# Level scores of a chunked gated recurrence: one 128x128 product a chunk, or two of 64 keys by 64 queries on separate column tiles

## The chip, the cores and the metric

The kernel runs on one core of a Trainium2 chip. The metric is the device time of one execution in microseconds (us). TensorE multiplies matrices into PSUM (the profile calls its products PE and its weight loads PEld), VectorE (DVE) and ScalarE (ACT) read PSUM and do elementwise work, GpSimd (POOL) works on SBUF alone, and SyncE (SP) issues most DMAs.

## The reference, cut to what matters

The program is one layer of a transformer-like block on 2048 latent tokens of width 1024 with a context of 256 tokens. One of its two head groups is a gated linear recurrence, run in both directions, with 4 heads of 128 channels:

```python
def chunk_gla(q, k, v, log_f, h0):
    # S_t = diag(f_t) S_{t-1} + k_t v_t^T,  o_t = S_t^T q_t
    ...
        b = jnp.cumsum(gc, axis=2)
        o_inter = jnp.einsum('bhtk,bhkv->bhtv', qc * jnp.exp(b), h)
        diff = b[:, :, :, None, :] - b[:, :, None, :, :]
        decay = jnp.where(mask, jnp.exp(jnp.where(mask, diff, 0.0)), 0.0)
        scores = jnp.einsum('bhtk,bhsk,bhtsk->bhts', qc, kc, decay)
        o = o_inter + jnp.einsum('bhts,bhsv->bhtv', scores, vc)
...
    o_f, h_f = chunk_gla(q, k_f, v, logf_f, h0_f)
    o_b, h_b = chunk_gla(flip_t(q), flip_t(k_b), flip_t(v), flip_t(logf_b), h0_b)
    o = rmsnorm(o_f + flip_t(o_b), hg_gain.reshape(HG_HEADS, 1, HG_DIM))
```

Around it stand an input projection (1024 to 3584 columns), a gated unit with a 128x128 mixing matrix, an output projection, and a gated MLP with a 3x3 convolution. All is computed in float32 accuracy.

## The kernel before, in words

**Stages.** The kernel first makes the modulation vectors and the context states, then runs the input projection for two halves of 1024 tokens, and beside it the recurrence (up to about 925 us), then the output projection, the MLP's up projection with the convolution, and the down projection. The large products are split in a high and a low part of type float32r (three products for one); those of the recurrence use plain float32, which TensorE runs as two passes, each with a weight load.

**The recurrence.** The function `hg` handles one head of one half: 1024 tokens as 8 chunks of 128 (`NCH`). It is called 8 times (2 halves, 4 heads). The scores inside a chunk are built by levels B = 1, 2, 4, ..., 64 (`LV`). At level B, two neighbouring blocks of B tokens look at each other: forward for one direction, backward for the other. The pair of blocks is 2B wide, so with B up to 32 a pair lies in the first or in the second 64 tokens of the chunk, and with B = 64 the two halves of the chunk look at each other. The tile `Q` holds the queries of both directions in two rows of 1024, and a level reads for each token the row that it needs. The tile `K` holds in its row 0 the keys that the level needs. A level's steps are

- 8 products `T.matmul(o, K[:, 0, chunk], view(Q, ...))`, one a chunk: 128 keys by 128 queries, contracted over 128 channels, four to a PSUM bank with the tag `sc` (two banks);
- for B below 64, `copy_predicated` on VectorE, one for each group of four chunks: it takes from the bank what the level's mask `msk` selects and puts it in the tile `sc` in SBUF. For B = 64 two ScalarE copies a group take the two off-diagonal quarters;
- `level_update` on VectorE, which multiplies `Q` by the decay totals `tot` of the level, `level_keys` on VectorE, GpSimd and ScalarE, which makes the keys of the next level in another `K` tile, and `next_tot`.

Level B = 1 is computed otherwise, as column sums of elementwise products with ones.

**Order.** The tile framework sets semaphores from what each instruction reads and writes, and may reorder instructions that are not kept in place by `pin`. The order of TensorE is mostly written out by hand: `run_banks` issues the projections (28 or so between two levels), and after each three products it calls `slot()`, which lets two queues of generators (`Pump`) go one step when they are due. `hg` is such a generator. What counts as due is reckoned by the planner's clock `T.t`, which the class `Tensor` moves on by an estimated price of each product; `yield 4.2` means that the next level is issued when 4.2 us of estimated products have been issued since. The background queue (`bg_q`: modulation blocks, the preparation of the output and down projections' weights, with their DMAs) uses the same clock.

Of the kernel before, what the change touches and what calls it, by code (L numbers as in the profile page):

```python
# [10 lines left out]
F32R = mybir.dt.float32r  # L11
# [5 lines left out]
DRAM = bass.MemoryType.DRAM  # L17

P = 128
D = 1024  # L20
NK = D // P
SEQ = 2048
TH = SEQ // 2
NCH = TH // P
CTX = 256
HW = 512
NH = 4
FF = 2816
NF = FF // P
GW = 64  # L30
# [9 lines left out]
def level_masks():  # L40
    i = np.arange(P)
    m = []
    for b in LV:
        same = (i[:, None] // (2 * b)) == (i[None, :] // (2 * b))
        opp = (i[:, None] // b) != (i[None, :] // b)
        m.append(same & opp)
    m.append(np.eye(P, dtype=bool))
    return np.ascontiguousarray(np.stack(m, 1).reshape(P, 8 * P).astype(np.float32))


def view(t, off, dims):

    return bass.AP(t.tensor, t.offset + off, [list(t.ap[0])] + [list(d) for d in dims])


class Tensor:
# [5 lines left out]
    def matmul(self, out, lhsT, rhs, **kw):  # L62
        n = 1
        for _, count in rhs.ap[1:]:
            n *= count
        self.t += n / 2400 + 0.0135 if rhs.dtype == F32R else 2 * max(0.112, n / 1200 + 0.005)
        return self.engine.matmul(out, lhsT, rhs, **kw)  # L67

    def transpose(self, out, in_, identity):
# [16 lines left out]
def tile_trunk(ctx, tc, x, c, cx, c_ctx, w_ada, b_ada, norm_mix, norm_ffn, w_in, hg_norm, sgu_g, sgu_b,  # L86
               w_sp, b_sp, w_out, w_up, conv_w, conv_b, w_down, norm_final, masks, out):
    nc = tc.nc
    V, S, G, T = nc.vector, nc.scalar, nc.gpsimd, Tensor(nc.tensor)
# [25 lines left out]

    g_d = dr.tile([2, D], F32, name="g_d")
    oT_d = [dr.tile([P, NK, TH], F32, name=f"oT{hh}") for hh in range(2)]
    xh_d = dr.tile([P, NK, TH], F32, name="xh_d")
    xl_d = dr.tile([P, NK, TH], F32, name="xl_d")
    wo_d = dr.tile([P, NK, 2, D], F32, name="wo_d")  # L120
    wd_d = [dr.tile([P, 2, D], F32, name=f"wd{j}") for j in range(NF // 2)]
    xn_d = [dr.tile([P, D], F32, name=f"xn{i}") for i in range(2 * NCH)]

# [68 lines left out]
    with es1:  # L192
# [8 lines left out]
        msk = pm.tile([P, 8, P], U8, name="msk")  # L201
# [4 lines left out]
        def bank(tag):  # L206
            return ps.tile([P, 512], F32, tag=tag, name=tag, bufs={"pj": 3, "sc": 2, "mi": 3}[tag])
# [7 lines left out]
        def raw_tile():  # L215
            return p1.tile([P, D], F32, tag="raw", name="raw", bufs=3)

# [123 lines left out]
        with tc.manual_schedule():  # L341
# [29 lines left out]
            for k in range(NK):  # L371
                for i in range(2):
                    o = (k % 2) * 256 + i * P
# [130 lines left out]
        def level_update(arr, W, B, tot, kk):  # L504

            n = W // (2 * B)
            nb = W // B
            o = view(arr, 0, [[2 * B, n], [W + B, 2], [1, B]])
            if kk:
                t = view(tot, nb + 1, [[2, n], [-(nb + 1), 2], [0, B]])  # L510
            else:
                t = view(tot, 1, [[2, n], [nb - 1, 2], [0, B]])
            if B < 4 and not kk:
                o = view(arr, 0, [[W + B, 2], [2 * B, n], [1, B]])
                t = view(tot, 1, [[nb - 1, 2], [2, n], [0, B]])
            V.tensor_mul(o, o, t)

        def next_tot(tot, W, B):
            nb = W // B
            od = B in (1, 4, 16, 64)  # L520
            t2 = ph.tile([P, 2 * (W // (2 if od else 4))], F32, tag=f"T{int(od)}", name="tot")
            t2 = t2[:, :nb].rearrange("p (d n) -> p d n", d=2)
            pin(V.tensor_mul(t2, tot[:, :, 0::2], tot[:, :, 1::2]))  # L523
            return t2
# [52 lines left out]
        def level_keys(K, B, tot, K2=None):  # L577

            W, nb = TH, TH // B
            K2 = K2 if K2 is not None else pk.tile([P, 2, W], F32, tag="K", name="K2", bufs=2, align_bytes=AL)  # L580
            if B == P // 2:
                n = W // (2 * B)
                src = [[2 * B, n], [B, 2], [1, B]]
                t = view(tot, nb + 1, [[2, n], [-(nb + 1), 2], [0, B]])
                V.tensor_mul(view(K2, 0, [[2 * B, n], [W + B, 2], [1, B]]), view(K, 0, src), t)
                S.copy(view(K2, W, [[2 * B, n], [B - W, 2], [1, B]]), view(K, W, src))
                return K2
            n = W // (4 * B)
            for row, (o, step, t0, ts) in enumerate(((0, 3 * B, nb + 1, 1 - nb), (B, B, 0, nb + 3))):
                src = [[4 * B, n], [step, 2], [1, B]]  # L590
                e = G if row and B > 1 else V
                keep = pin if B == 1 else lambda i: i
                e.tensor_mul(view(K2, row * W + o, src), view(K, o, src), view(tot, t0, [[4, n], [ts, 2], [0, B]]))  # L593
                o2, step2 = (B, B) if row == 0 else (0, 3 * B)
                src = [[4 * B, n], [step2, 2], [1, B]]
                keep(S.copy(view(K2, row * W + o2, src), view(K, W + o2, src)))
            return K2
# [59 lines left out]
        for h in range(NH):  # L657
            F, K, vt = sets[h % 2]
# [129 lines left out]
        def column_sums(to, hi, lo):  # L788

            T.matmul(to, ones_r, hi, start=True, stop=False)  # L790
            T.matmul(to, ones_r, lo, start=False, stop=True)

        def hg(hh, h, F, K, qs, vt, sgt):
            Q = ph.tile([P, 2, TH], F32, tag="Q", name="Q", align_bytes=AL)
# [10 lines left out]
            pbs = [bank("sc") for g in range(2)]  # L805
# [3 lines left out]
            sc = ph.tile([P, NCH, P], F32, tag="S", name="sc")  # L809
# [15 lines left out]
            yield 3.2  # L825
            tot = F
            for l, B in enumerate(LV):
                dims = [[2 * B, P // (2 * B)], [TH + B, 2], [1, B]]
                if B < 4:
                    dims = [[TH + B, 2], [2 * B, P // (2 * B)], [1, B]]  # L830
                if B == P // 2:
                    dims = dims[1:]
                for g in range(0, NCH, 4):
                    pb = bank("sc")
                    if B == 1:
                        column_sums(pb, knh[g // 4], knl[:, g * P:g * P + 512])
                    for i in range(4) if B > 1 else ():
                        off = (g + i) * P
                        o = pb[:, i * P:(i + 1) * P]
                        if B < 4:  # L840
                            o = view(pb, i * P, [[B, 2], [2 * B, P // (2 * B)], [1, B]])
                        T.matmul(o, K[:, 0, off:off + P], view(Q, off, dims), start=True, stop=True)
                    if B == P // 2:
                        pq = pb.rearrange("p (c t) -> p c t", t=P)
                        S.copy(sc[:B, g:g + 4, B:], pq[:B, :, B:])
                        S.copy(sc[B:, g:g + 4, :B], pq[B:, :, :B])
                        continue
                    V.copy_predicated(sc[:, g:g + 4, :], view(msk, l * P, [[0, 4], [1, P]]),
                                      pb.rearrange("p (c t) -> p c t", t=P))
                level_update(Q, TH, B, tot, False)  # L850
                K, K2 = level_keys(K, B, tot, K2), None
                tot = next_tot(tot, TH, B)
                yield 4.2
# [3 lines left out]
            for d in range(2):  # L857
                for g in range(0, TH, 512):
                    pt = bank("mi")
                    for i in range(4):  # L860
                        o = g + i * P
# [29 lines left out]
            for g in range(0, NCH, 4):  # L891
                po = bank("mi")
                for i in range(4):
                    ch = g + i
                    sl = slice(ch * P, (ch + 1) * P)
                    o = po[:, i * P:(i + 1) * P]
# [127 lines left out]
        def head(hh, h):  # L1024
# [31 lines left out]
            def post():  # L1056
                hg_q.add(marked(hg(hh, h, t["F"], t["K"], t["qs"], t["vt"], t["sgt"]), (hh, h, "end")))
                if hh == 1:
                    hg_q.add(deferred(h))
# [102 lines left out]
        i = len(seq) - 4  # L1162
# [11 lines left out]
        for n in range(2):  # L1174
            sl = slice(n * 512, n * 512 + 512)
            for k in LATE:
                t = wo[k][:, :, sl]
# [11 lines left out]
    pb = ctx.enter_context(tc.tile_pool(name="pb", bufs=1, reuse_waits="tile"))  # L1189
# [11 lines left out]
    def zbank():  # L1201
        turn[1] += 1
        return ps2.tile([P, 512], F32, tag=f"uz{turn[1] % 2}", name="uz")
# [75 lines left out]
    for n, (u, i) in enumerate(prods):  # L1279
        m = units.index(u) + 2  # L1280
# [12 lines left out]
    with tc.tile_pool(name="po", bufs=1, reuse_waits="tile") as po:  # L1293
# [59 lines left out]
        for t, (hh, g) in enumerate(tiles):  # L1353
# [12 lines left out]
            o = ops.pop(t)  # L1366
# [33 lines left out]
    B = [[xah[:, i] if i < NR else None, xal[:, i] if i < NR - 1 else None] for i in range(7)]  # L1400
# [186 lines left out]
    for n, (u, i) in enumerate(prods):  # L1587
# [10 lines left out]
        p = zbank() if i == 1 else u.z if i in (4, 6) else u.x  # L1598
        hi, lo = u.A[i]
        order = [(k, 0, t) for k in range(4) for t in range(2)] + [(k, 1, 0) for k in range(4)]  # L1600
        for m, (k, w, t) in enumerate(order):
            T.matmul(p, (hi, lo)[w][:, k, :], B[i][t][:, k, :], start=(m == 0 and i in (0, 1, 4)),
                     stop=(m == len(order) - 1), skip_group_check=True)
# [36 lines left out]
    V = Kept(nc.vector, pin)  # L1640
# [191 lines left out]
    for n in range(3, 7 * NJ - NB):  # L1832
        q, j = divmod(n, NJ)
# [54 lines left out]
```

## Time and profile before

| | |
|---|---|
| median of three runs | 2432.91 us (2429.09 to 2433.07) |
| profiled execution, its time and its span | 2434.68 us, span 2432.9 us |
| TensorE products, weight loads (busy) | 2398.8 us, 1991.8 us |
| VectorE, ScalarE, GpSimd (busy) | 1658.5 us, 1045.1 us, 868.8 us |
| level products `sc<-Q,K` | 768 passes, 94.2 us busy |
| masked copies `sc<-msk,sc` | 96, 67.7 us busy |

Rows of groups read: line of the kernel, engine, operation, tile written <- tiles read, shape, xcount | busy time in us, mean ns of one | idle time of the engine before them and what ended it. For TensorE `128*64` would be rows by columns of the array. In order of time the columns are start, busy time, engine, line, operation; rows of the same kind that follow each other are merged with xcount. Durations of products overlap each other, so the pace is read from starts. The line of a product is that of the helper in `Tensor`, so products are told apart by their tiles.

### The profile page before, as it was taken

The page shows a single profiled execution, that of the slowest core. Times are in us where ns is not written, and L with a number is a line of the kernel's source. Part 1 is how long each engine was busy: PE and PEld are TensorE (multiplying, and loading weights), DVE is VectorE, ACT ScalarE, POOL GpSimd, SP SyncE. Part 2 cuts the span into 40 slices and gives each one's busy share as a digit, 9 for nine tenths or more (in the row PEclk, how much of TensorE's full clock was granted, in tenths as well). Part 3 has the DMA queues.
Part 4 walks back from the last instruction along what each step waited for, and adds up shares of the span by engine and source line. Part 5 has one row for each costly group of instructions (what it writes and reads, how often), then busy time and mean ns, then how long its engine had stood idle before and what let it go on. Part 6 is the DMA issues. An engine that isn't in the chain of part 4 may idle for free.

```text
span 2432.9 us, 32291 instructions
## 1 busy us (share of the span) xinstructions
PE 2398.8 (99%) x11711; PEld 1991.8 (82%) x11711; DVE 1658.5 (68%) x2251; ACT 1045.1 (43%) x1803; POOL 868.8 (36%) x788
## 2 busy tenths in 40 slices
PE   8999999999999999999999999999999999999998
PEld 5887887888888887887788888888888888888887
DVE  5757795755786786566596666639866673676876
ACT  4554344443444443454554444434445443332243
POOL 1021110110121122000688778787888870000002
PEclk9999999999999999999999999999999999999999
DMA  8365444463355234678922222563222239834745
GB/s 308 119 205 166 148 143 165 140 225 107 119 193 171 91 105 145 217 218 254 301 85 89 93 81 91 185 230 97 86 94 84 86 108 387 285 118 147 229 152 199
DMA packets 304046, 393.28 MB, mean 162 GB/s; under 512 B 32634, under 2 KB 215682, under 8 KB 300814
## 3 DMA queue, kind: packets, MB, share of 16 engines
q1 hardware_dynamic: 300596, 390.46, 48.0%
q8 instruction: 92, 1.51, 0.2%
q10 hardware_dynamic: 3289, 0.76, 0.1%
q14 instruction: 69, 0.56, 0.1%
HBM read 283.60 MB, written 107.55 MB: 161 GB/s over the span
## 4 chain that ended last, share of the span: by engine, by line
PE 47%; issue 2%; POOL 1%; ACT 0%; DVE 0%; DMA 0%; POOLq 0%; SPq 0%; ACTq 0%
PE ux L67 19%; PE dn L67 15%; PE uz L67 14%; POOL rr L1748 0%; DMA raw<-in_w_up_dram 0%; POOL Al L135 0%; POOL ra L1747 0%; POOL ra L1745 0%; ACT jk L1736 0%; POOL raw L1262 0%; DVE odd L82 0%; POOL raw L1260 0%; DVE dn L1453 0%; POOL s L1258 0%; POOL fl L1258 0%
## 5 line engine op out<-in xcount | busy, mean ns | idle before, releaser
L1453 DVE SCALAR_TENSOR_TENSOR dn<-gp,taps,dn 128x1024 f32<-128x1024 f32 x352 | 448.3, 1285 | 97.7 <-ACT dn L1450 93.3
L67 PE MATMUL dn<-thl,mhl 128*128 128x512 f32 x1680 | 381.0, 389 | 0.0
L67 PEld LDWEIGHTS dn<-thl,mhl 128*128 128x128 f32 x1680 | 315.2, 188 | 65.6 <-issue 0.2
L135 POOL TENSOR_TENSOR Al<-raw,Ah 128x512 fp32r<-128x512 f32 x264 | 341.2, 1309 | 69.4 <-ACT Ah L134 41.0
L67 PE MATMUL pj<-xh,whi 128*128 128x512 f32 x896 | 362.6, 405 | 0.0
L67 PE MATMUL pj<-xl,whi 128*128 128x512 f32 x896 | 352.6, 393 | 0.0
L67 PE MATMUL pj<-xh,wlo 128*128 128x512 f32 x896 | 351.2, 392 | 0.4 <-DVE wlo L135 0.4
L134 ACT CAST Ah<-raw 128x512 fp32r<-128x512 f32 x264 | 163.0, 620 | 240.5 <-PE ux L67 125.0
L67 PE MATMUL ux<-xah,Ah 128*128 128x512 f32 x528 | 205.7, 390 | 0.3 <-ACT keep L1517 0.3
L67 PEld LDWEIGHTS pj<-xh,wlo 128*128 128x128 f32 x896 | 168.6, 188 | 35.9 <-DVE wlo L135 0.8
L67 PEld LDWEIGHTS pj<-xh,whi 128*128 128x128 f32 x896 | 168.9, 189 | 33.7 <-issue 3.5
L67 PEld LDWEIGHTS pj<-xl,whi 128*128 128x128 f32 x896 | 169.2, 189 | 30.8 <-DVE xl L254 0.8
L67 PE MATMUL dn<-wo,o 128*128 128x512 f32 x768 | 182.4, 394 | 0.0
L67 PE MATMUL uz<-yf,Ah 128*128 128x512 f32 x704 | 174.0, 389 | 0.0
L593 POOL TENSOR_TENSOR K<-K,tot 128x512 f32<-128x512 f32 x40 | 61.5, 1538 | 302.7 <-DVE tot L523 156.2
L67 PEld LDWEIGHTS dn<-wo,o 128*128 128x128 f32 x768 | 142.1, 188 | 29.0
L67 PE MATMUL ux<-yf,Ah 128*128 128x512 f32 x528 | 155.4, 389 | 0.0
L67 PEld LDWEIGHTS uz<-yf,Ah 128*128 128x128 f32 x704 | 132.1, 188 | 27.4
L67 PE MATMUL ux<-xah,Al 128*128 128x512 f32 x528 | 141.8, 390 | 1.3 <-POOL Al L135 1.3
L67 PE MATMUL ux<-xal,Ah 128*128 128x512 f32 x352 | 137.0, 389 | 0.0
L1745 POOL TENSOR_SCALAR ra<-ss 128x1 f32<-128x1 f32 x8 | 3.2, 397 | 359.5 <-ACT jk L1736 359.5
L135 DVE TENSOR_TENSOR wlo<-raw,whi 128x1024 fp32r<-128x1024 f32 x67 | 82.5, 1232 | 67.7 <-ACT whi L134 66.3
(344 smaller groups left out, 4449.9 us busy)
## 6 DMA issues: line engine op xcount, KB each, us to landing
raw<-in_w_up_dram SPq DMA_DIRECT2D x88, 512.0 KB, 3.6
mr<-m SPq DMA_DIRECT2D x85, 512.0 KB, 5.4
raw<-in_w_in_dram SPq DMA_DIRECT2D x68, 512.0 KB, 4.8
sT<-wd SPq DMA_DIRECT2D x88, 256.0 KB, 5.0
raw<-in_w_ada_dram SPq DMA_DIRECT2D x32, 512.0 KB, 4.5
yf<-yd SPq DMA_DIRECT2D x14, 1024.0 KB, 10.0
m<-cv SPq DMA_DIRECT2D x22, 544.0 KB, 2.7
raw<-in_w_down_dram SPq DMA_DIRECT2D x22, 512.0 KB, 3.6
```

Of the source, the lines that this page charges most:

```text
L67: return self.engine.matmul(out, lhsT, rhs, **kw)
L134: keep(S.copy(hi, raw))
L135: (eng or G).tensor_sub(lo, raw, hi.bitcast(F32))
L593: e.tensor_mul(view(K2, row * W + o, src), view(K, o, src), view(tot, t0, [[4, n], [ts, 2], [0, B]]))
L1453: V.scalar_tensor_tensor(out=cr, in0=gt[:, t // 3:t // 3 + RH, t % 3:t % 3 + GW], scalar=taps[:, t * NF + f:t * NF + f + 1], in1=cr, op0=A ...
L1745: G.tensor_scalar(out=a, in0=ss, scalar1=plus, scalar2=None, op0=ALU.add)
```

## The change

For each chunk and level above B = 1 the one product becomes two, r = 0 and 1: 64 keys (from e = 64 r) by 64 queries, written to the 64 partitions of PSUM from e on. Its output columns are those of the same half of the chunk for B below 64, and of the other half for B = 64; the two other quarters of the 128x128 block are not computed any more. An output that starts at partition 64 uses the upper half of TensorE's columns, one at partition 0 the lower half. Both banks of a level are asked for first, then come the products of both groups of chunks, then the copies. The masked copy of a group becomes two, each of the quarter on the diagonal (64 partitions by 4 x 64 elements); for B = 1 and B = 64 the copies stay. The planner's price of a float32 product now has its constant part scaled with the number of weight columns.

```diff
+HB = 64
...
-        self.t += n / 2400 + 0.0135 if rhs.dtype == F32R else 2 * max(0.112, n / 1200 + 0.005)
+        m = lhsT.ap[-1][1] / P
+        self.t += n / 2400 + 0.0135 if rhs.dtype == F32R else 2 * max(0.112 * m, n / 1200 + 0.005)
...
             for l, B in enumerate(LV):
-                dims = [[2 * B, P // (2 * B)], [TH + B, 2], [1, B]]
-                if B < 4:
-                    dims = [[TH + B, 2], [2 * B, P // (2 * B)], [1, B]]
-                if B == P // 2:
-                    dims = dims[1:]
+                pbs = [bank("sc") for g in range(2)]
                 for g in range(0, NCH, 4):
-                    pb = bank("sc")
+                    pb = pbs[g // 4]
                     if B == 1:
                         column_sums(pb, knh[g // 4], knl[:, g * P:g * P + 512])
                     for i in range(4) if B > 1 else ():
-                        off = (g + i) * P
-                        o = pb[:, i * P:(i + 1) * P]
-                        if B < 4:
-                            o = view(pb, i * P, [[B, 2], [2 * B, P // (2 * B)], [1, B]])
-                        T.matmul(o, K[:, 0, off:off + P], view(Q, off, dims), start=True, stop=True)
+                        for r in range(2):
+                            off, e = (g + i) * P, r * HB
+                            c = e if B < HB else HB - e
+                            dims = [[2 * B, HB // (2 * B)], [TH + B, 2], [1, B]]
+                            d = e
+                            if B < 4:
+                                dims = [[TH + B, 2], [2 * B, HB // (2 * B)], [1, B]]
+                            if B == HB:
+                                dims, d = [[1, B]], (TH + B) * (1 - r)
+                            o = pb[e:e + HB, i * P + c:i * P + c + HB]
+                            if B < 4:
+                                o = view(o, 0, [[B, 2], [2 * B, HB // (2 * B)], [1, B]])
+                            T.matmul(o, K[:, 0, off + e:off + e + HB], view(Q, off + d, dims), start=True, stop=True)
+                for g in range(0, NCH, 4):
+                    pq = pbs[g // 4].rearrange("p (c t) -> p c t", t=P)
                     if B == P // 2:
-                        pq = pb.rearrange("p (c t) -> p c t", t=P)
                         S.copy(sc[:B, g:g + 4, B:], pq[:B, :, B:])
                         S.copy(sc[B:, g:g + 4, :B], pq[B:, :, :B])
                         continue
-                    V.copy_predicated(sc[:, g:g + 4, :], view(msk, l * P, [[0, 4], [1, P]]),
-                                      pb.rearrange("p (c t) -> p c t", t=P))
+                    if B == 1:
+                        V.copy_predicated(sc[:, g:g + 4, :], view(msk, l * P, [[0, 4], [1, P]]), pq)
+                        continue
+                    for e in (0, HB):
+                        q = slice(e, e + HB)
+                        V.copy_predicated(sc[q, g:g + 4, q], view(msk[q], l * P + e, [[0, 4], [1, HB]]), pq[q, :, q])
```

## The prediction

> **What bounds the kernel now.** I read the page first, then the stretch in which the level scores run, then the groups by shape, and last the order of time around single bursts. From the page:
>
> ```profile
> span 2432.9 us, 32291 instructions
> PE 2398.8 (99%) x11711; PEld 1991.8 (82%) x11711; DVE 1658.5 (68%) x2251; ACT 1045.1 (43%) x1803; POOL 868.8 (36%) x788
> PE   8999999999999999999999999999999999999998
> PEclk9999999999999999999999999999999999999999
> ```
>
> TensorE is busy in every slice at its full granted clock. So what TensorE saves anywhere ends the program earlier, unless another engine makes it wait. The heads of the recurrence lie between 215 and 925 us; the busy time of each engine in that stretch, and what TensorE waited for before level scores there:
>
> ```profile
> 215.00:925.00 710.00, 701.33 (x3888) 599.13 (x3886) 518.48 (x774) 297.04 (x561) 111.04 (x99) 1.00 0.43 144
> PE sc L67 <- DVE K L593: 2.5, 4, 0.9
> PE sc L67 <- DVE Q L516: 1.4, 2, 0.9
> ```
>
> The columns are length, then PE, PEld, DVE, ACT, POOL, clock, DMA share and GB/s. TensorE idles 8.7 us of 710 here, and only six waits, 3.9 us, stand before level scores. VectorE is at 73%, so it has room. The groups that the change touches:
>
> ```profile
> L67 PE MATMUL sc<-Q,K 128*128 128x128 f32 x768 | 94.2, 275 | 3.9 <-DVE K L593 2.5 <-DVE Q L516 1.4
> L67 PEld LDWEIGHTS sc<-Q,K 128*128 128x128 f32 x768 | 92.4, 191 | 9.5 <-issue 4.2 <-ACT whi L134 1.1 <-PE mi L71 1.1
> L848 DVE COPY_PREDICATED sc<-msk,sc 128x512 f32<-128x512 uint8 x96 | 67.7, 735 | 13.4 <-PE sc L67 13.3
> ```
>
> Six levels (B=2 to 64) of eight heads with eight chunks are 384 products; the trace has 768 rows, so an f32 product is two passes, each with its own weight load. 768 rows in 48 levels are 16 passes a level. Durations overlap, so a price has to come from starts. One such burst in order of time, TensorE first, then its weight loads (start, busy, what):
>
> ```profile
> 268.67 0.39 PE L67 MATMUL pj<-xl,whi 128*128 128x512 f32 x1
> 268.89 0.39 PE L67 MATMUL pj<-xh,wlo 128*128 128x512 f32 x1
> 269.12 1.95 PE L67 MATMUL sc<-Q,K 128*128 128x128 f32 x16
> 270.82 0.48 PE L67 MATMUL pj<-xh,whi 128*128 128x512 f32 x1
> 271.14 0.40 PE L67 MATMUL pj<-xl,whi 128*128 128x512 f32 x1
> 271.37 0.39 PE L67 MATMUL pj<-xh,wlo 128*128 128x512 f32 x1
> ...
> 268.90 1.98 PEld L67 LDWEIGHTS sc<-Q,K 128*128 128x128 f32 x16
> ```
>
> The 16 passes already stand in one row. From their first start to the next projection is 1.70 us, and that projection is followed after 0.32 us where 0.23 is usual. A burst therefore takes 1.79 us out of the projections, 0.112 us a pass, and 48 bursts cost 86 us, 3.5% of the run. That is the most the change could touch.
>
> **The change part by part.**
>
> *Streaming.* Each pass of 128 queries becomes two of 64 queries. At half the columns I price one at 0.056 us, half of 0.112. A level has 32 of them in place of 16, so one after the other they cost 32 x 0.056 = 1.79 us, the same as now. A gain comes only if the lower tile (partitions 0 to 63) and the upper one (64 to 127) work at the same time.
>
> *Weight loads.* Would they limit it? In this row the products have two columns to stream:
>
> ```profile
> 35.94 1.05 PE L67 MATMUL sc<-ones_r,acc 128*128 128x2 f32 x8
> L67 PE MATMUL sc<-ones_r,acc 128*128 128x2 f32 x16 | 2.1, 254 | 0.0
> ```
>
> Eight of them take 1.05 us and the last 0.25, so they start (1.05 - 0.25)/7 = 0.114 us apart, though there is next to nothing to stream: loading 128 columns of f32 weights alone holds the pace. Loads and streams are thus equal limits today, and the change loads the same 128 columns a pass in two halves. It halves the burst only if loads of the two tiles overlap as well as streams. No row shows two products on different column tiles. The bounds are full overlap (16 steps of 0.056 us, 0.90 us a burst) and none (32 steps, 1.79).
>
> I take overlap. The program's order helps: within a tile the second pass waits for the first, but the next instruction is for the other tile, so from the second pass on one pass of each tile can run beside one of the other: 17 steps instead of 16, 17 x 0.056 = 0.95 us. And the nearest rows on loads, those of the one-column products below, show two loads in hand (of one tile) before the first of their products is done.
>
> By the Trainium skill, TensorEngine Tiling (Array Packing), Key Properties, different tiles can execute weight loads and products in parallel; by that sentence the sum is the one I take. The trace has no such pair, so it neither bears this out nor refutes it.
>
> *Going into the narrow mode and out.* The nearest rows are the products with one weight column, between projections of 128 (TensorE, then loads):
>
> ```profile
> 368.97 0.39 PE L67 MATMUL pj<-xl,whi 128*128 128x512 f32 x1
> 369.19 0.39 PE L67 MATMUL pj<-xh,wlo 128*128 128x512 f32 x1
> 369.51 1.02 PE L67 MATMUL mi<-acc,ones_r 128*1 128x512 f32 x2
> 370.46 0.50 PE L67 MATMUL pj<-xh,whi 128*128 128x512 f32 x1
> 370.80 0.39 PE L67 MATMUL pj<-xl,whi 128*128 128x512 f32 x1
> 371.03 0.39 PE L67 MATMUL pj<-xh,wlo 128*128 128x512 f32 x1
> ...
> 369.51 0.09 PEld L67 LDWEIGHTS mi<-acc,ones_r 128*1 128x1 f32 x2 [0.35 <-issue]
> 370.46 0.19 PEld L67 LDWEIGHTS pj<-xh,whi 128*128 128x128 f32 x1 [0.86 <-issue]
> 370.57 0.19 PEld L67 LDWEIGHTS pj<-xl,whi 128*128 128x128 f32 x1
> L67 PE MATMUL mi<-acc,ones_r 128*1 128x512 f32 x8 | 4.1, 590 | 0.0
> ```
>
> In: 0.32 us from 369.19 to 369.51 where 0.23 is usual, 0.09 lost. Out: the second pass starts at 369.51 + 1.02 - 0.59 = 369.94, 0.43 after the first; the projection follows 0.52 later, again 0.09 lost. That projection's load starts only with it (370.46), not under the product before, so the next comes after 0.34 instead of 0.23: 0.11 lost. I add 0.06 for the first 64-column load of a burst, half of that 0.11. Together 0.35 us for each of 48 bursts, 16.8 us in all. The ends are 0 (if two tiles of 64 need no change of mode) and 0.35. Both groups of chunks stand in one row before and after, so that edit changes nothing here.
>
> By the same page of the Trainium skill and the same section, changing the tiling mode drains TensorE. The three lost pieces above agree with that; without the rule the sum would lose its 16.8 us.
>
> *Sum on TensorE.* A burst goes from 1.79 to 0.95 + 0.35 = 1.30 us: 0.49 us less, 48 times, 23.5 us.
>
> *Copies.* For B=2 to 32 two masked copies of 128x512 become four of 64x256: 80 instructions become 160; those of B=1 and the ScalarE copies of B=64 stay. What VectorE did after a burst, and a group with 256 columns that also reads PSUM:
>
> ```profile
> 265.35 1.34 DVE L848 COPY_PREDICATED sc<-msk,sc 128x512 f32<-128x512 uint8 x2
> 266.59 1.21 DVE L516 TENSOR_TENSOR Q<-Q,tot 128x1024 f32<-128x1024 f32 x1
> L251 DVE TENSOR_SCALAR xfl<-mi,a,s 128x256 f32<-128x256 f32 x32 | 16.9, 538 | 8.4 <-PE mi L71 4.3 <-ACT sp L253 3.1 <-POOL sp L254 0.8
> ```
>
> Two copies take 1.34 us; the second adds 1.34 - 0.74 = 0.60. The bounds for four halves are 1.34 (half the price) and 4 x 0.53 = 2.1 (the 256-column row, 16.9/32). I take 1.5, near the first, since these copies follow each other without idle time: +0.16 us for 40 levels, 6 to 7 us of VectorE. VectorE's 73% covers it. Behind the copies in VectorE's queue stands the update of Q, and for that the next burst waits. Also, a shorter burst hides less of the first copies: its second half was 0.9 us and becomes about 0.5, so the update comes some 0.6 us later, counted from the burst's end. Here it ended at 267.8 and the next burst began at 269.12, so 1.3 us of slack cover it; of 48 bursts six had none. 6 x 0.6 is 3.6 us; the ends are 0 and that, I take 2.
>
> *Planner.* Its price of a product goes from 0.224 to 2 x 0.1167 = 0.233, which is 0.075 us a level and 3.6 us over the heads. Later steps, with their DMAs on SP's queue and GpSimd's work, are issued slightly earlier relative to the projections. I cost it at nothing; it could move the 8.7 us of waits either way.
>
> **Sum.** The profiled execution took 2434.7 us with a span of 2432.9; its time is 1.8 above the median of the runs, 2432.9. 2434.7 - 23.5 + 2 = 2413.2; against the median 2411. With its own bounds (no price for the mode: 16 us less; a third of the overlap lost or more waiting: 9 us more) this case reaches from 2395 to 2420.
>
> **Rivals.**
>
> *Tiles take turns (the other sign).* If the weight loads of the two tiles queue on one path, 32 steps of 0.056 us remain, 1.79 us, and the change of mode comes on top: +0.35 us a burst, 16.8 us, and 2 for the waits: 2452 against the median, and 2456 if a half pass costs 0.058, as the planner has it. For it: the row with two columns, where loads alone hold 0.114 us. Against it: two loads in hand at 369.51. The point that decides is the mean step: 1.79 = 0.35 + 32 x 0.045, so overlap must bring a half pass below 0.045 us to gain anything.
>
> *Loads exposed.* If a load could not run under a product of the same rows, each half pass would pay load and stream, 0.11 us: 32 x 0.112 + 0.35 - 1.79 = 2.1 us a burst, 102 us, 2537. Against it: at 268.90 a load starts 0.01 us after a product that uses all 128 rows.
> The Trainium skill, TensorE: Matmul & The Clock Gate, Part 3, states that loads overlap products in flight only when the row group differs; that would give this rival. The row at 268.90 speaks against it, at least for untiled products.
>
> *VectorE takes the gain back.* If every burst, not six, waited 0.6 us for the update of Q, 29 us would go and the time would be 2438, no gain. It decides when the slack falls under 0.6 us in most bursts; 42 of 48 without any wait and the 1.3 us above speak against it.
>
> **How the numbers follow.** Overlap 0.52; taking turns 0.33; partial overlap or VectorE's return, around no change, 0.10; exposed loads 0.05. A difference under 0.2%, 4.9 us, cannot be told from no change here. Faster 0.55 (overlap and a share of the partial case), same 0.07, slower 0.38. The two large cases have different signs, so the range spans both, 2398 to 2456; overlap's own is 2395 to 2420.
>
> **What would show it.** Starts of level passes: 32 rows in about 0.95 us, with lower and upper tile in pairs, if right; 1.8 us if they take turns; 3.6 if loads are exposed. The projection after a burst followed by 0.34 us in place of 0.32, and 0.09 us lost on either side, would confirm the price of the mode. Copies of 64x256 near 0.47 us, and waits of TensorE for Q and K near 6 us in place of 3.9. The prediction is wrong if loads of two column tiles do not overlap.

## The result, and the profile after

The changed kernel takes 2419.8 us (median; 2418.6 to 2422.8) against 2433.0 before: a ratio of 0.9949 with a 95% interval of 0.9932 to 0.9966, so 12 to 13 us less. By the length of its bursts TensorE saved as much as forecast, some 24 us; some 10 us of that were lost again, to longer waits and to a lower granted clock behind two of them (last section). Page and stretch of the heads after the change (the columns of the stretch as before):

```profile
span 2418.3 us, 33888 instructions
PE 2376.4 (98%) x12479; PEld 1954.8 (81%) x12479; DVE 1671.6 (69%) x2331; ACT 1045.5 (43%) x1803; POOL 869.0 (36%) x788
215.00:915.00 700.00, 682.91 (x4680) 564.80 (x4679) 536.65 (x862) 298.80 (x562) 113.05 (x99) 1.00 0.44 146
```

TensorE's busy time fell by 22.4 us, the span by only 14.6: its idle time grew by 7.8 us. In the stretch of the heads it idles 17.1 us of 700, where it was 8.7 of 710. VectorE has 13 us more work. A burst of level products in order of time, and the first of its weight loads' rows:

```profile
435.07 0.39 PE L69 MATMUL pj<-xl,whi 128*128 128x512 f32 x1
435.30 0.39 PE L69 MATMUL pj<-xh,wlo 128*128 128x512 f32 x1
435.62 1.15 PE L69 MATMUL sc<-Q,K 128*64 128x64 f32 x32
436.70 0.50 PE L69 MATMUL pj<-xh,whi 128*128 128x512 f32 x1
437.03 0.39 PE L69 MATMUL pj<-xl,whi 128*128 128x512 f32 x1
...
435.62 1.01 PEld L69 LDWEIGHTS sc<-Q,K 128*64 128x64 f32 x32 [0.35 <-issue]
```

From the first pass to the next projection it is now 1.08 us, 1.70 before, though there are 32 passes instead of 16. In the single records the passes stand in pairs, 0.007 us apart, and the pairs follow each other every 0.058 us: lower and upper column tile work side by side, loads included. The groups that changed, and what TensorE waited for:

```profile
L69 PE MATMUL sc<-Q,K 128*64 128x64 f32 x1536 | 55.9, 226 | 9.8 <-DVE Q L518 3.8 <-DVE K L595 3.3 <-DVE tot L525 1.3
L860 DVE COPY_PREDICATED sc<-msk,sc 64x256 f32<-64x256 uint8 x160 | 71.4, 446 | 7.5 <-PE sc L69 4.7
L856 DVE COPY_PREDICATED sc<-msk,sc 128x512 f32<-128x512 uint8 x16 | 11.0, 726 | 0.2 <-PE sc L69 0.2
```

Idle time before level products is 9.8 us, 3.9 before, and the masked copies take 82.4 us in place of 67.7. In VectorE's order of time the four quarter copies of a level, and the update of Q behind them:

```profile
797.44 1.83 DVE L860 COPY_PREDICATED sc<-msk,sc 64x256 f32<-64x256 uint8 x4
799.28 1.23 DVE L518 TENSOR_TENSOR Q<-Q,tot 128x1024 f32<-128x1024 f32 x1
```

Four copies of half the columns take 1.83 us; two whole ones took 1.34. Nothing overlaps: 1.83/4 is 0.46, the full length of one, and Q starts when the last has ended. Before, the second copy added only 0.60 of its 0.74.

### The profile page after: what moved, and what is told of

The parts are those of the page before. It is cut to its first block, busy times and chain, and to the rows that moved or that the text cites. A ratio compares the mean times of both kernels' runs of the same rounds, so it can differ in the third digit from the quotient of the medians.

```text
span 2418.3 us, 33888 instructions
## 1 busy us (share of the span) xinstructions
PE 2376.4 (98%) x12479; PEld 1954.8 (81%) x12479; DVE 1671.6 (69%) x2331; ACT 1045.5 (43%) x1803; POOL 869.0 (36%) x788
## 3 DMA queue, kind: packets, MB, share of 16 engines
q8 instruction: 98, 1.61, 0.3%
## 4 chain that ended last, share of the span: by engine, by line
PE 49%; issue 2%; POOL 1%; DMA 1%; DVE 0%; ACT 0%; SPq 0%; POOLq 0%; ACTq 0%; DVEq 0%
PE ux L69 19%; PE dn L69 16%; PE uz L69 14%; DMA raw<-in_w_up_dram 1%; POOL rr L1759 0%; DMA yf<-yd 0%; POOL Al L137 0%; DMA xn<-cv 0%; POOL ra L1758 0%; POOL ra L1756 0%; DVE fl L137 0%; PE ux L73 0%; ACT jk L1747 0%; ACT yst L136 0%; POOL raw L1273 0%
```

## The experiments

The theory after seeing this trace: the two tiles overlap and save 24 us; the quarter copies make VectorE's level chain longer, and TensorE waits for it. The rivals: the waits come from the planner's drift and a new order of instructions, or the shorter burst hides less of the copies whatever these cost. Ratios are against the kernel before.

**Both quarters of one half first** (`e1_halves_in_turn`), the changed kernel with

```diff
-                    for e in (0, HB):   # inside the loop over g
-                        q = slice(e, e + HB)
-                        V.copy_predicated(sc[q, g:g + 4, q], view(msk[q], ...), pq[q, :, q])
+                    for e in (0, HB):   # once, when both banks are there
+                        q = slice(e, e + HB)
+                        for gg, src in ((0, pq0), (4, pq)):
+                            V.copy_predicated(sc[q, gg:gg + 4, q], view(msk[q], ...), src[q, :, q])
```

> The changed kernel with the four quarter copies of a level in another order: both of partitions 0 to 63, then both of 64 to 127. Theory (copies): a VectorE instruction that starts on another partition half than the one before it is not overlapped with it; four copies then take about 0.33 + 0.46 + 0.33 + 0.46 = 1.6 us in place of 1.83, VectorE's busy time falls by some 8 to 10 us, and TensorE's waits in the recurrence by a third: 2414 to 2418 us. Rival (order): the waits come from the planner's drift and from another order of the background work, not from the copies' price; then the copies may get shorter, and the time stays at 2420 or moves either way by up to 5 us. Rival (no hold): the order makes no difference to the copies, 1.83 us stay.

Measured: 2418.2 us, ratio 0.9932 (0.9918 to 0.9945), which overlaps the changed kernel's interval. The framework reorders copies, and kept the old order in about half of the levels. The semaphore waits in the records tell which: the second bank is waited for by the second copy in the new order, by the third in the old. Two levels of this run, the first with the new order, the second with the old one:

```profile
704.62 1.58 DVE L864 COPY_PREDICATED sc<-msk,sc 64x256 f32<-64x256 uint8 x4
706.21 1.23 DVE L518 TENSOR_TENSOR Q<-Q,tot 128x1024 f32<-128x1024 f32 x1
...
795.70 1.83 DVE L864 COPY_PREDICATED sc<-msk,sc 64x256 f32<-64x256 uint8 x4
797.55 1.22 DVE L518 TENSOR_TENSOR Q<-Q,tot 128x1024 f32<-128x1024 f32 x1
```

Of the 31 levels whose four copies stand together in this run, 15 have the new order. In 14 of these the second and the fourth copy start 0.1 us before the one ahead ended, and only the change of half is held up; in the old order, and in all 31 such levels of the changed kernel, every copy is held up. So the price of the change of half is shown, 1.58 against 1.83 us. VectorE's busy time fell by 4.0 us, not by the 8 to 10 that the theory had; the effect on the time, 1.6 us in the medians, is not clear of noise.

The Trainium skill, VectorE: DVE Perf Modes, section on two Vector instructions with no wait between them, says that an instruction whose operand starts in another group of 32 partitions than that of the last access waits until all earlier ones have finished. The trace agrees: 0.46 us a copy across the halves, some 0.35 within one.

**Whole copies** (`e2_full_copies`), products as in the change:

```diff
+            pbs = [bank("sc") for g in range(2)]
             for l, B in enumerate(LV):
-                pbs = [bank("sc") for g in range(2)]
...
-                    for e in (0, HB):
-                        q = slice(e, e + HB)
-                        V.copy_predicated(sc[q, g:g + 4, q], view(msk[q], ...), pq[q, :, q])
+                    V.copy_predicated(sc[:, g:g + 4, :], view(msk, l * P, [[0, 4], [1, P]]), pq)
```

> The changed kernel with the two masked copies of 128x512 of the kernel before; the two banks are taken once a head, so that the quarters that are no longer computed hold old values, which the mask leaves out. Theory (copies): VectorE is back at 0.735 us a copy and 1.34 us a level, 15 us less busy time, TensorE's idle time between 215 and 915 us falls from 17 to about 9 to 11 us, and nearly all of the 24 us that the products save arrive: 2409 to 2413 us. Rival (cover): the shorter burst hides less of the copies whatever they cost, the waits stay near 17 us: 2418 to 2421. Rival (order): anything between.

Measured: 2409.2 us, ratio 0.9895 (0.9879 to 0.9911), clear of the changed kernel's interval. The same groups and the stretch:

```profile
L69 PE MATMUL sc<-Q,K 128*64 128x64 f32 x1536 | 55.4, 225 | 2.4 <-DVE K L595 2.3
L855 DVE COPY_PREDICATED sc<-msk,sc 128x512 f32<-128x512 uint8 x96 | 66.2, 732 | 10.5 <-PE sc L69 10.4
215.00:915.00 700.00, 689.77 (x4758) 571.69 (x4757) 521.98 (x797) 304.17 (x572) 113.92 (x100) 1.00 0.45 150
```

The idle time before level products is 2.4 us, less than before the change; in the stretch it is 10.2. Of the 24.4 us that the products save, 23.9 arrive. The burst is as short as in the changed kernel, so a short burst alone is not the cause, and the rival of the cover falls as it was put; the run with eight passes in a row (below) shows that cover matters all the same. This edit also keeps the two banks for a whole head, and no run has that without whole copies.

**Quarter copies alone** (`e3_quarters_only`), the kernel before with

```diff
-                    V.copy_predicated(sc[:, g:g + 4, :], view(msk, l * P, [[0, 4], [1, P]]), ...)
+                    for e in (0, HB):   # for B from 2 to 32
+                        q = slice(e, e + HB)
+                        V.copy_predicated(sc[q, g:g + 4, q], view(msk[q], l * P + e, [[0, 4], [1, HB]]), pq[q, :, q])
```

> The kernel before with the quarter copies alone: products of 128 keys by 128 queries, planner as before. Theory (copies): four copies take 1.83 us in place of 1.34, VectorE has about 15 us more, and TensorE waits 3 to 10 us more: 2436 to 2443 us. Rival (cover or order): without the shorter burst and the planner's drift the copies cost nothing: 2433, within 0.2%.

Measured: 2444.1 us, ratio 1.0039 (1.0025 to 1.0054), 11 us slower, one above the range of the theory.

```profile
L68 PE MATMUL sc<-Q,K 128*128 128x128 f32 x768 | 94.8, 276 | 9.0 <-DVE K L594 3.8 <-DVE Q L517 3.3 <-ACT whi L135 1.1
L855 DVE COPY_PREDICATED sc<-msk,sc 64x256 f32<-64x256 uint8 x160 | 71.4, 446 | 8.7 <-PE sc L68 6.2
```

The same copies at the same price raise the waits before level products from 3.9 to 9.0 us with the old products and the old planner. TensorE's busy time is 5 us longer too (2403.8 us); stretches of a lower granted clock (last section), two more here than in the trace of the kernel before, make an estimated 3.4 us of that. In these two pairs of kernels, this one against the kernel before and the changed kernel against whole copies, quarter copies cost 11 us.

**The planner's old price** (`e4_price_as_before`), the changed kernel with

```diff
-2 * max(0.112 * m, n / 1200 + 0.005)
+(0.112 if n == HB else 2 * max(0.112 * m, n / 1200 + 0.005))
```

> The changed kernel, quarter copies and all, with the planner's price of a half product set to 0.112 us, so that a chunk counts 0.224 us as before the change. Theory (copies): the planner's 3.6 us of drift are no part of the loss, TensorE's waits in the recurrence stay near 17 us and the time at 2417 to 2423 us. Rival (order): the waits came from later steps being issued at other places; with the old price they go back to about 9 us and the time falls to 2409 to 2413.

Measured: 2419.9 us, ratio 0.9943 (0.9931 to 0.9955), as the changed kernel. Waits before level products were 11.8 us. The drift of 3.6 us is no part of the loss.

**The planner's measured price** (`e6_price_measured`), whole copies with 0.0585 in that place.

> The kernel with full copies (two tiles, two copies of 128x512, banks taken once a head) with the planner's price of a half product set to what the trace shows, 0.0585 us instead of 0.117, so that the planner's clock no longer runs ahead by 0.94 us a level. Theory: the background steps that are due by this clock come a little later and closer to what they were priced for; TensorE's idle time of 28 us falls by 0 to 3 us: 2406 to 2410. Rival: a slower clock puts more projections between steps, some VectorE work then meets the level chain elsewhere, and the time moves up by as much.

Measured: 2409.8 us, ratio 0.9899 (0.9887 to 0.9910): as with whole copies, no difference to be told.

**Eight passes of a tile in a row** (`e5_turns`), the changed kernel with

```diff
-                    for i in range(4) if B > 1 else ():
-                        for r in range(2):
+                    for r in range(2) if B > 1 else ():
+                        for i in range(4):
```

> The changed kernel with the products of a bank in another order: four for the lower column tile, then four for the upper, so eight passes of one tile stand in a row. Theory (neighbours overlap): a pass runs beside the other tile's only if they stand next to each other; a burst is then near 32 x 0.056 = 1.8 us, three borders between tiles saving about 0.06 each, 0.6 to 0.7 us more than now, 48 times: 2448 to 2454 us, slower than before. Rival (deep look-ahead): TensorE finds the other tile's passes behind the eight and the burst stays at 1.08 us: 2420.

Measured: 2428.6 us, ratio 0.9974 (0.9964 to 0.9985), between the two. A burst of it:

```profile
443.34 1.54 PE L69 MATMUL sc<-Q,K 128*64 128x64 f32 x32
444.81 0.50 PE L69 MATMUL pj<-xh,whi 128*128 128x512 f32 x1
```

It takes 1.47 us instead of 1.08. In the single records the first five passes of a burst stand 0.06 us apart or more, and the sixth starts 0.007 us behind the fifth, in all 48 bursts: it must be the upper tile's first, with three passes of the lower still ahead of it. The pass that reports the first bank done, its sixteenth in the program, is mostly the nineteenth to start, so passes do start out of the program's order. TensorE overlaps a few passes ahead, not eight. Both theories were half right.

The time says something else as well. Bursts that are 0.39 us longer would cost 18.7 us, but the kernel is only 8.8 us slower than the changed one, with the same quarter copies (82.4 us of VectorE):

```profile
L69 PE MATMUL sc<-Q,K 128*64 128x64 f32 x1536 | 73.8, 228 | 3.4 <-DVE K L595 1.6 <-DVE Q L518 0.8 <-ACT whi L136 0.8
```

The idle time before level products is 3.4 us instead of 9.8. The time is about that of the kernel with whole copies plus the longer bursts, 2409.2 + 18.7 = 2427.9, so by this estimate the quarter copies cost next to nothing here. Their loss is thus no fixed price: it depends on the slack that is left when they run. Why they cost 11 us beside the still longer bursts of `e3_quarters_only` is not settled.

**One tile only** (`e9_one_tile`), whole copies and

```diff
-o = pb[e:e + HB, i * P + c:i * P + c + HB]
+o = pb[:HB, i * P + c:i * P + c + HB]
```

> The kernel with full copies, but both half products of a chunk are written to partitions 0 to 63, side by side in the bank, so all 32 passes of a level use the lower column tile; the scores of the upper 64 keys are left out. Same instructions, same copies. Theory (the gain is overlap of two tiles): the passes take turns, 32 x 0.058 = 1.86 us, 0.93 more a burst, 45 us: 2450 to 2456, as the rival of the prediction had it, slower than before by about 0.9%. Rival (narrow passes are simply cheap): the burst stays at 1.08 us and the time at 2409.

Measured: 2454.1 us, ratio 1.0083 (1.0070 to 1.0097).

```profile
454.29 2.08 PE L69 MATMUL sc<-Q,K 128*64 128x64 f32 x32
456.30 0.50 PE L69 MATMUL pj<-xh,whi 128*128 128x512 f32 x1
```

The burst takes 2.01 us, 0.93 more, which is 16 steps of 0.058: the same 32 passes on one tile take turns. 48 x 0.93 = 44.6 us, and the median is 44.8 above that with whole copies. The gain on TensorE is the overlap of two column tiles.

**Four tiles of 32** (`e7_tiles_of_32`), whole copies and, for B up to 16,

```diff
+                    W = 32 if B < 32 else HB
                     for i in range(4) if B > 1 else ():
-                        for r in range(2):
-                            off, e = (g + i) * P, r * HB
+                        for r in range(P // W):
+                            off, e = (g + i) * P, r * W
...
-                            o = pb[e:e + HB, i * P + c:i * P + c + HB]
+                            o = pb[e:e + W, i * P + c:i * P + c + W]
```

> The kernel with full copies, and for B up to 16 four products of 32 keys by 32 queries on four column tiles (B = 32 and 64 stay at two). Theory (tiles are independent as far as TensorE looks ahead): 64 passes of 32 columns, four beside each other, take 16 steps of about 0.03 to 0.04 us; such a burst falls from 0.93 to 0.5 to 0.65 us, 32 bursts save 9 to 14 us: 2395 to 2400 us. Rival (issue): passes cannot start closer than they do now (0.058 us for two, 0.029 each), so 64 of them take 1.9 us, and 32 bursts cost 30 us: 2440. Rival (between): only two or three tiles get going at once, the burst stays at 0.9 us: 2409.

Measured: 2404.6 us, ratio 0.9878 (0.9865 to 0.9892).

```profile
436.56 0.76 PE L69 MATMUL sc<-Q,K 128*32 128x32 f32 x64
437.25 0.50 PE L69 MATMUL pj<-xh,whi 128*128 128x512 f32 x1
```

64 passes in 0.69 us: four tiles overlap too. 32 bursts save 0.39 us each, 12.4 in all. The theory's 2395 to 2400 was missed: the time fell by 4.6 against whole copies (the two intervals overlap a little), while TensorE's idle time between its products rose from 28.0 to 33.4 us (27.1 before the change, 34.9 with it), so some 8 us were given back, 5.4 of them as idle time.

**Later levels** (`e10_later_levels`, four tiles; `e11_after_later_levels`, the changed kernel): `yield 4.2` becomes `yield 5.0`.

> The kernel with four tiles of 32 up to B = 16 and full copies, with each level issued after 5.0 us of planned products instead of 4.2. Theory (the rest of the loss is the level chain on VectorE being late): three or four more projections stand between two bursts, TensorE's waits before level products (idle time 33 us in all) go back to about the 27 us of before, and the time falls by 4 to 6 us: 2398 to 2401. Rival (the heads get too long): each head's recurrence lasts 5.6 us more, the next steps are forced earlier in the head that follows, and the waits move to the transposes and the states: 2405 or above.

Measured: 2400.0 us, ratio 0.9855 (0.9838 to 0.9872), the fastest kernel here and inside the theory's range; the idle time between products is 29.3 us, where about 27 were expected. The intervals with and without the later levels overlap a little.

> The changed kernel itself, quarter copies and all, with 5.0 us of planned products between levels instead of 4.2. Theory (copies make the chain late, and lateness is what costs): 0.8 us more of cover is above the 0.5 us that four quarter copies take more than two whole ones, the waits before level products fall by half, and the time to 2411 to 2415, most of what whole copies bring. Rival (VectorE's load, not the chain, is the cost): the 15 us of VectorE work stay and so does the time, 2418 to 2422.

Measured: 2417.3 us, ratio 0.9924 (0.9912 to 0.9937): of some 10 us at most 2 or 3 came back, and the idle time before level products is still 8.0 us. The theory's 2411 to 2415 was missed. Whether it is the longer chain or VectorE's 15 us of added work as such that makes TensorE wait is not settled; whole copies remove both.

## Why the prediction was right, and where it was not

**The sum on TensorE held.** The step was 0.058 us for a pair (0.056 taken). The passes went from 1.79 us to 16 steps, 0.93, with no extra step for the lag, as pairs stand together from the first. The price of the mode: 0.09 going in (435.30 to 435.62 is 0.32, usual 0.23), 0.05 for the first narrow load (the second pair starts 0.106 us behind the first, later ones 0.058), 0.09 going out (0.15 from the last pair in place of 0.058), 0.11 for the load that is not hidden (0.33 instead of 0.23 behind 436.70): 0.34, where the sum had 0.35. From 435.62 to 436.70 is 1.08, so a burst costs 0.09 + 1.08 + 0.11 = 1.28 us, against the 1.30 of the sum: 24.4 us saved, 23.5 forecast.

**Tiles take turns** was the right price for the wrong case: the one-tile kernel, which has whole copies, came out at 2454 where the rival said 2452 to 2456. Passes on one tile do take 0.058 us each in turn; two tiles have two such paces, loads included. No row of the kernel before showed which of the two it would be, and the prediction gave overlap 0.52 against 0.33. The range of 2398 to 2456 spans both cases, so that the time lies in it says little.

**Loads exposed** did not occur: in the changed kernel's records each load behind the second pair's starts 0.002 to 0.003 us behind a product that uses the same 128 rows. The sentence of the Trainium skill (TensorE: Matmul & The Clock Gate, Part 3) that loads overlap products in flight only when the row group differs is not borne out, neither for untiled products nor for column tiles.

**The step that failed is the copies' price.** I took 1.5 us for four, near half the price each, "since these copies follow each other without idle time". That row showed two copies on the same partitions; it said nothing of copies that change halves. Measured are 1.83 us, the overlap being lost at each change, and 14.7 us of VectorE work in place of 6 to 7.

**With it went the waits.** I took 2 us, six bursts that come 0.6 us late. Idle time rose by 7.8 us, and 11 of 48 bursts waited, not six. The rival in which VectorE takes the gain back was thus true for some 10 of 24 us, more than a third. It needed slack under 0.6 us in most bursts; 37 of the 48 did not wait at all, but some of the others waited far longer than 0.6. VectorE ahead of the worst wait, then TensorE before and behind it:

```profile
801.56 1.24 DVE L525 TENSOR_TENSOR tot<-tot 128x128 f32<-128x128 f32 x1
802.83 0.69 DVE L1032 SCALAR_TENSOR_TENSOR qs<-pj,sig 128x512 f32<-128x512 f32 x1
803.44 1.72 DVE L1024 TENSOR_TENSOR raw<-raw,g 128x1024 f32<-128x1024 f32 x1
805.08 1.80 DVE L860 COPY_PREDICATED sc<-msk,sc 64x256 f32<-64x256 uint8 x4
806.90 1.22 DVE L518 TENSOR_TENSOR Q<-Q,tot 128x1024 f32<-128x1024 f32 x1
```

```profile
801.02 1.15 PE L69 MATMUL sc<-Q,K 128*64 128x64 f32 x32
802.10 0.50 PE L69 MATMUL pj<-xh,whi 128*128 128x512 f32 x1
...
805.41 0.39 PE L69 MATMUL pj<-xh,wlo 128*128 128x512 f32 x1
808.27 1.68 PE L69 MATMUL sc<-Q,K 128*64 128x64 f32 x32 [2.47 <-DVE Q L518]
809.88 0.80 PE L69 MATMUL pj<-xh,whi 128*128 128x512 f32 x1
810.48 0.63 PE L69 MATMUL pj<-xl,whi 128*128 128x512 f32 x1
```

The burst ahead gives way to the projections at 802.10, but its copies start only at 805.08: other VectorE work, at last a background step on the down projection's weights (`raw`), holds them back. The copies hold Q back, and the next burst starts 0.15 us after Q has ended at 808.12. The longer copies are some 0.5 us of this wait of 2.47; the rest is what stood ahead of them. With whole copies the longest wait from 795 to 830 us is 0.28 us.

**The planner** was priced at nothing, and two kernels with other prices bear that out. The 3.6 us of drift was too small a figure, though: with passes at 0.058 us a pair the planner's clock runs ahead of TensorE by 0.94 us a level. With whole copies that costs nothing (2409.8 against 2409.2 us); with quarter copies the measured price was not run.

The forecast of 2411 is within 2 us of the kernel with whole copies, 2409; the measured 2420 lies at the upper end of the range given for overlap.

## What to carry to other kernels

Where products need only blocks on the diagonal, column tiles give f32 products twice the pace on two tiles and more on four, if neighbours in the program's order use different tiles; each visit to the narrow mode costs about 0.3 us, so visits should be long. Do not cut the VectorE work that reads the result the same way without measuring it: here a whole copy under a mask, with banks kept so that the unused quarters hold old values, was 11 us cheaper than quarter copies on alternating partition halves. A saving on the busiest engine is worth what the engines that feed it can follow; look at the slack of the chain behind it first.

## What the runs showed of the hardware

- Two column tiles load f32 weights and stream at once: passes 0.007 us apart, a pair every 0.058 us. In the order with eight passes of a tile in a row, TensorE started a pass of the other tile with three passes of the first still ahead of it, not with more.
- A long wait of TensorE can cost more than its length. Granted clock in three stretches of the changed kernel around the wait of 2.47 us above (third column from the end):

```profile
800.00:805.00 5.00, 5.00 (x50) 3.98 (x49) 4.87 (x6) 1.14 (x2) 2.75 (x2) 1.00 0.32 96
807.50:810.00 2.50, 1.73 (x33) 1.64 (x33) 2.21 (x5) 0.00 (x0) 0.00 (x0) 0.73 0.33 102
810.00:812.00 2.00, 2.00 (x5) 1.62 (x6) 1.96 (x5) 1.14 (x2) 1.08 (x1) 0.50 0.65 187
```

  Behind it the clock was 0.50, a burst took 1.61 us instead of 1.08, and projections stood 0.42 apart instead of 0.23. Between 215 and 925 us the changed kernel has two such stretches, 3.4 us each, from 808.7 and from 911.1, behind waits of 2.47 and 2.48 us; with whole copies there is none. At half the clock the two lose an estimated 3.4 us, nearly all of the 3.7 us that the changed kernel's TensorE is busier than with whole copies (2376.4 against 2372.7). Not every long wait is followed by one: with the planner's old price a wait of 2.50 us before 807.5 was not (clock 1.00 from 805 to 812).
